# The recurrent branch's projection over both token halves by seven half-size products in rounds, with the first half's output projection ahead of the last two rounds

## The chip, the core and the metric

The kernel runs on one NeuronCore of a Trainium2 chip. The engines are TensorE (PE in the profile; PEld is its weight load), VectorE (DVE), ScalarE (ACT), GpSimd (POOL) and SyncE (SP, which here only issues DMAs). The metric is the device time of one execution in microseconds. Two kernels are compared by the medians of several executions of each.

## The reference

One layer of a decoder trunk on 1024 tokens of width 1024. The part that is changed lies between the three branches of the token mixer and the output projection:

```python
y_pool = pool_branch(...) @ w_proj_pool[l]
y_mem = mem_attention(...) @ w_proj_mem[l]
y_rwkv = rwkv_branch(...) @ w_proj_rwkv[l]
gates = jax.nn.sigmoid(z_gate.reshape(B, S, N_BRANCH, D) + gate_b[l])
merged = gates[:, :, 0] * y_pool + gates[:, :, 1] * y_rwkv + gates[:, :, 2] * y_mem
x = x + rms_norm(merged @ w_o[l], norm_mix_post[l])
```

`w_proj_rwkv` and `w_o` are 1024 x 1024. A convolutional feed-forward (width 2816, twice) follows.

## The kernel before

Activations lie with channels on the 128 partitions and tokens along the free axis; 1024 channels are 8 blocks, and the 1024 tokens are two halves of 512. For precision each factor is split into a high part in fp32r and a low part (`split`, L123, for activations; `split_w`, L127, for weights: ACT casts `whi` at L132, POOL makes `wlo` at L139), and a block of 128 x 128 weights against 128 x 512 activations takes three matmuls (`mm3`: L180 high by high, L181 high weights by low activations, L182 low weights by high activations). `gemm` sums 8 such blocks into one PSUM bank: 24 matmuls for 128 output channels of one half. `load_w` brings weights in tiles of two blocks through buffers of two classes that alternate from one load to the next: three raw tiles, four `whi` and four `wlo` in each class.

Stages around the change, in the program's order:

- the memory branch's projection (`w_pmem`, L1062 to L1070): 8 x 2 products of 12 matmuls, each multiplied with its gate into `pm` (L1070);
- the pooling branch's projection (`w_ppool`, to L1080): the same, added to `pm`;
- `yr` (L1093) loads the recurrent branch's output from DRAM, 8 blocks over all tokens, and `split` makes `yh`, `yl`;
- `merge(n, js)`: for half n and output block j, `gemm` of `w_prwkv[j]` against `yh`, `yl`, the gate's sigmoid, then on DVE L1109 (gate times PSUM), L1110 (plus `pm`) and the split into `mgh` (L124, ACT) and `mgl` (L125, DVE);
- `wo_gemm(n, js)`: the output projection; each product is copied out on DVE (L1332) and its square summed (ACT L1306, DVE L1307). The first two output blocks are woven (`two_gemms`), so that the last input block is needed late;
- `wo_residual(n)`: a matmul with ones for the norm (L1312), then for each of 8 blocks a scaling (L1355), a sum with the input (L1357), a store, and the sum of squares;
- `wo_norm(n)`: the feed-forward's norm and split into `h2h`, `h2l`; then the feed-forward's up projection.

The driver runs `merge` for half 0, `wo_gemm(0)`, `merge` for half 1 with `wo_residual(0)` woven into it, and `wo_gemm(1)` with `wo_norm(0)` inside. Every engine works its queue in order. The order within a queue is set when the program is built, from the order of the code and a scheduler's own estimate of times; a tile's buffer is reused when its last reader is done, and an instruction that waits for that holds up what stands behind it on its engine.

In the later stage (`up_pairs`) the kernel already uses the scheme that the change brings here: a 2 x 2 product of blocks by seven products and sums in place of eight products (its low halves of weights are L1172).

## Time and profile before

| | us |
|---|---|
| median of 3 runs (1959.63 to 1962.59) | 1961.81 |
| profiled execution | 1961.22 |
| its span in the trace | 1959.5 |
| TensorE busy | 1912.1 |
| DVE, ACT, POOL busy | 1361.5, 1044.3, 791.9 |

The span is what the trace covers, from the first to the last instruction. A row of a group reads: line, engine, operation, output and inputs with their shapes, count, then busy time in us and mean ns, then the engine's idle time just before them and what ended it. A row of a line's or tile's instructions gives min/median/max in ns and the first and last start in us. Rows of stretches give busy us (and instructions) for PE, PEld, DVE, ACT and POOL, the granted clock of TensorE, the DMA engines' share and GB/s.

### The profile page before, as it was taken

How to read it: one execution, taken by the hardware profiler on the slowest of the kernel's cores; microseconds unless marked ns; L12 is line 12 of the kernel's file. 1: busy time of each engine (PE TensorE's matmuls, PEld its weight loads, DVE VectorE, ACT ScalarE, POOL GpSimd, SP SyncE). 2: the span in 40 equal slices, each digit the busy share in tenths (PEclk: the TensorE clock that was granted, in tenths of full speed). 3: DMA queues.
4: the chain of work that ended last, by engine and by line, in shares of the span. 5: the costliest groups of instructions: out<-in, count | busy, mean ns of one | idle time of the engine just before them, and what ended most of it. 6: DMA issues, size and time to landing. Idle time of an engine off the chain costs nothing.

```text
span 1959.5 us, 33751 instructions
## 1 busy us (share of the span) xinstructions
PE 1912.1 (98%) x12204; PEld 1543.9 (79%) x12204; DVE 1361.5 (69%) x2022; ACT 1044.3 (53%) x2158; POOL 791.9 (40%) x867
## 2 busy tenths in 40 slices
PE   8999999999999999999999999999999999999997
PEld 6777777777777777777888888888888888888886
DVE  8677567677677435546884443689798888877798
ACT  7685385385384244445665244546554545454544
POOL 4422221321321211111223365565599888822441
PEclk9999999999999999999999999999999999999999
DMA  4325235225239668966318343644322222289775
GB/s 162 129 71 177 96 86 175 90 86 175 94 107 279 190 207 279 300 215 212 108 59 274 123 144 111 225 150 133 122 76 87 81 87 76 97 241 227 172 182 146
DMA packets 269639, 296.26 MB, mean 151 GB/s; under 512 B 18336, under 2 KB 219168, under 8 KB 266400
## 3 DMA queue, kind: packets, MB, share of 16 engines
q1 hardware_dynamic: 248480, 271.56, 43.2%
q0 software_dynamic: 11856, 14.16, 4.4%
q10 hardware_dynamic: 9136, 8.39, 1.4%
q8 instruction: 96, 1.57, 0.3%
q14 instruction: 71, 0.58, 0.1%
HBM read 207.00 MB, written 87.03 MB: 150 GB/s over the span
## 4 chain that ended last, share of the span: by engine, by line
PE 77%; DVE 8%; DMA 6%; ACT 4%; issue 3%; POOL 1%; SPq 0%; ACTq 0%; POOLq 0%; DVEq 0%
PE psg L180 14%; PE psg L182 14%; PE psg L181 14%; PE psf L182 5%; PE psf L180 5%; PE psf L181 5%; PE psd L181 3%; PE psd L182 3%; PE psd L180 3%; PE py L770 2%; DMA wraw<-in_w_in 1%; PE ps L605 1%; DVE tb L651 1%; DVE tb L653 1%; DMA d_bv<-kv 1%
## 5 line engine op out<-in xcount | busy, mean ns | idle before, releaser
L139 POOL TENSOR_TENSOR wlo<-wraw,whi 128x256 fp32r<-128x256 f32 x464 | 410.7, 897 | 833.8 <-ACT whi L132 772.7
L180 PE MATMUL psg<-hh,whi 128*128 128x512 f32 x928 | 380.1, 410 | 12.2 <-ACT whi L132 5.9
L182 PE MATMUL psg<-hh,wlo 128*128 128x512 f32 x928 | 368.0, 397 | 2.7 <-POOL wlo L139 2.2
L181 PE MATMUL psg<-hl,whi 128*128 128x512 f32 x928 | 367.8, 396 | 0.7 <-DVE hl L266 0.6
L132 ACT CAST whi<-wraw 128x256 fp32r<-128x256 f32 x472 | 181.2, 402 | 236.2 <-PE psg L181 99.1
L180 PEld LDWEIGHTS psg<-hh,whi 128*128 128x128 f32 x928 | 175.0, 189 | 60.1 <-ACT whi L132 11.2
L182 PEld LDWEIGHTS psg<-hh,wlo 128*128 128x128 f32 x928 | 175.0, 189 | 44.8 <-POOL wlo L139 7.2
L181 PEld LDWEIGHTS psg<-hl,whi 128*128 128x128 f32 x928 | 175.3, 189 | 40.5 <-issue 4.5
L1172 POOL TENSOR_TENSOR wt<-a,wt 128x256 fp32r<-128x256 f32 x136 | 155.6, 1168 | 35.1 <-ACT wt L1171 35.1
L181 PE MATMUL psd<-f,u 128*128 128x512 f32 x292 | 113.9, 390 | 0.2 <-DVE f L1588 0.2
L180 PE MATMUL psd<-f,u 128*128 128x512 f32 x292 | 113.2, 391 | 0.8 <-ACT f L1584 0.8
L182 PE MATMUL psd<-f,u 128*128 128x512 f32 x292 | 113.7, 389 | 0.0
L182 PE MATMUL psf<-h2h,wt 128*128 128x512 f32 x272 | 105.9, 389 | 0.0
L181 PE MATMUL psf<-h2l,wt 128*128 128x512 f32 x272 | 105.8, 389 | 0.0
L180 PE MATMUL psf<-h2h,wt 128*128 128x512 f32 x272 | 105.8, 389 | 0.0
L1186 DVE SCALAR_TENSOR_TENSOR d<-z,pv,d 128x1023 f32<-128x1023 f32 x68 | 101.2, 1491 | 2.1
L1172 POOL TENSOR_TENSOR wt<-s,wt 128x256 fp32r<-128x256 f32 x68 | 80.0, 1197 | 3.8 <-ACT wt L1171 2.6
L180 PE MATMUL psf<-t,wt 128*128 128x512 f32 x204 | 79.4, 389 | 0.0
L181 PE MATMUL psf<-t,wt 128*128 128x512 f32 x204 | 79.4, 389 | 0.0
L182 PE MATMUL psf<-t,wt 128*128 128x512 f32 x204 | 79.4, 389 | 0.0
L1184 ACT ACTIVATE d<-z,pv 128x1024 f32<-128x1024 f32 x34 | 42.4, 1246 | 65.3 <-DVE z L1266 49.8
L1171 ACT CAST wt<-a 128x256 fp32r<-128x256 f32 x136 | 50.6, 404 | 41.3 <-POOL wt L1172 25.9
(432 smaller groups left out, 4565.7 us busy)
## 6 DMA issues: line engine op xcount, KB each, us to landing
wraw<-in_w_in SPq DMA_DIRECT2D x176, 128.0 KB, 2.3
a<-in_w_fup SPq DMA_DIRECT2D x128, 128.0 KB, 2.3
d_ar<-AR SPq DMA_DIRECT2D x24, 512.0 KB, 3.7
d_zg<-st SPq DMA_DIRECT2D x48, 256.0 KB, 3.7
ring<-d_ar SPq DMA_DIRECT2D x8, 1536.0 KB, 10.5
wraw<-in_w_fup SPq DMA_DIRECT2D x80, 128.0 KB, 2.4
fraw<-d_f SPq DMA_DIRECT2D x33, 256.0 KB, 4.2
d_rb<-RB SPq DMA_DIRECT2D x16, 512.0 KB, 3.9
```

The source lines that it names most:

```text
L132: i = A.copy(hi, src)
L139: (V if lo_on_dve[0] else G).tensor_tensor(lo, src, hi.bitcast(F32), op=ALU.subtract)
L180: first = PE.matmul(ps, wh, xh, start=start, stop=False)
L181: PE.matmul(ps, wh, xl, start=False, stop=False)
L182: last_mm[0] = PE.matmul(ps, wl, xh, start=False, stop=stop).ins
L605: PE.matmul(ps[:, c], BK[i][up, c0 + c], AR[up, i, 1:3, t], start=True, stop=True)
L651: V.tensor_tensor(tm, X[:, s + 1:, s:s + 1].broadcast_to([P, n, m]), S[:, s:s + 1, 0:m].broadcast_to([P, n, m]), op=ALU.mult)
L770: m = PE.matmul(out_, l, r, **kw)
L1171: A.copy(w[0][:, us], src[u])
L1172: low = eng.tensor_tensor(w[1][:, us], src[u], w[0][:, us].bitcast(F32), op=ALU.subtract)
L1184: A.activation(d, z, AF.Identity, scale=col("cw2", j), bias=col("cb", j))
L1186: V.scalar_tensor_tensor(d[:, n:], z[:, :T - n], col(cw, j), d[:, n:], op0=ALU.mult, op1=ALU.add)
```

## The change

The weights (output blocks 0 to 3 and 4 to 7, input blocks 0 to 3 and 4 to 7) and the recurrent output (input blocks, token halves) are taken as 2 x 2 matrices of quarters. Seven products of quarters, each a round r = 0 to 6 with four output blocks p = 0 to 3 of 12 matmuls, give all four result quarters after sums. Rounds 0, 1 and 4 use plain quarters of the weights; rounds 2, 3, 5 and 6 use sums that are made at run time (`merge_weights`: L1158 on POOL, L1159 on DVE, L1163 on POOL; `later_weights`: L1147 and L1148 on POOL), from raw blocks of 128 x 512 in five buffers named `sw`. The activation panels are quarters of `ys` ("a" and "c" are the first half's blocks 0 to 3 and 4 to 7, "b" and "d" the second half's) or differences of them; the `A` tiles of rounds 0 and 1 are taken over by the panels of rounds 3 and 4 (`big_panels`). The weights of a product are prepared three products ahead (`rounds`).

Rounds 0 and 1 are woven, then rounds 2, 3 and 4: 20 products, after which half 0 is complete. Then comes `wo_gemm(0)` with `known_part` and `later_weights` woven in, then rounds 5 and 6 (8 products) with `wo_residual(0)` beside them, then `wo_gemm(1)`, which now takes the input blocks in the order 4 to 7, 0 to 3, and copies its results out on ACT. The tiles of the `at` pool are now halves of 512 tokens.

```diff
+    y_ctx = ExitStack()
+    yp = y_ctx.enter_context(tc.tile_pool(name="yp", bufs=1, side="right"))
+    ys = {}
+
+    for k in range(4):
+        for nm, e, h in (("a", 0, 0), ("c", 4, 0), ("b", 0, 512), ("d", 4, 512)):
+            ys[nm, k] = yp.tile([P, 512], F32, name=f"y{nm}{k}", tag=f"y{nm}{k}")
+            SP.dma_start(ys[nm, k], d_y[e + k][:, h:h + 512])
+    big = [yp.tile([P, 4, 512], FR, name=f"yp{m}", tag=f"A{m}") for m in range(4)]
     for j in range(8):
+        if j % 2:
+            k = j // 2
+            split(ys["a", k], big[0][:, k], big[1][:, k], V)
+            split(ys["c", k], big[2][:, k], big[3][:, k], V)
+            V.tensor_tensor(ys["a", k], ys["b", k], ys["a", k], op=ALU.subtract)
+            V.tensor_tensor(ys["b", k], ys["d", k], ys["b", k], op=ALU.subtract)
+            G.tensor_tensor(ys["c", k], ys["c", k], ys["d", k], op=ALU.subtract)
+            G.tensor_tensor(ys["c", k], ys["c", k], ys["a", k], op=ALU.add)
         ws = load_w(w_ppool[j], 4)
...
+    def gated_sum(j, n, src, add, eng):
+
+        gt = gts[j, n]
+        V.tensor_tensor(gt, src, gt, op=ALU.mult)
+        V.tensor_tensor(gt, gt, add, op=ALU.add)
+        mgh[j, n] = half_tile(j, n, "mgh")
+        mgl[j, n] = pmp.tile([P, 512], FR, name=f"mgl{j}{n}", tag=f"n{2 * j + n}")
+        split(gt, mgh[j, n], mgl[j, n], eng)
+
+    def known_part(j):
+
+        c = result(j, 1)
+        later(V.tensor_tensor(c, c, gts[j, 1], op=ALU.mult), last_mm[0])
+        V.tensor_tensor(c, c, pm[j][1], op=ALU.add)
...
+    def raw_weights(j, k0):
+        w = mq.tile([P, 4, P], F32, name="sw", tag="sw", bufs=5)
+        SP.dma_start(w, w_prwkv[j][:, k0:k0 + 4])
+        return w
+
+    def later_weights(p):
+
+        s1[p], y = raw_weights(4 + p, 0), raw_weights(4 + p, 4)
+        later(G.tensor_tensor(s1[p], s1[p], y, op=ALU.add), last_mm[0])
+        G.tensor_tensor(kept[p], raw_weights(p, 4), kept[p], op=ALU.subtract)
+
+    def merge_weights(r, p):
+
+        plain_ = {0: (p, 0), 1: (p, 4), 4: (4 + p, 4)}.get(r)
+        if plain_:
+            return load_w(w_prwkv[plain_[0]][:, plain_[1]:plain_[1] + 4], 4)
+        if r == 2:
+            x, y, z = raw_weights(4 + p, 0), raw_weights(4 + p, 4), raw_weights(p, 0)
+            src = kept[p] = mq.tile([P, 4, P], F32, name=f"S{p}")
+            G.tensor_tensor(src, x, y, op=ALU.add)
+            V.tensor_tensor(src, src, z, op=ALU.subtract)
+            corner[0] = z, x
+        elif r == 3:
+            src, y = corner[0]
+            G.tensor_tensor(src, src, y, op=ALU.subtract)
+        else:
+            src = (s1 if r == 5 else kept)[p]
...
+        if r == 0:
+            A.copy(result(p, 0), ps)
+            A.copy(u2, ps)
+        elif r in (1, 4):
+            j = p if r == 1 else z
+            c = result(j, 0)
+            V.tensor_tensor(c, c, ps, op=ALU.add)
+            gated_sum(j, 0, c, pm[j][0], V)
+        elif r == 2:
+            V.tensor_tensor(u2, u2, ps, op=ALU.add)
+        elif r == 3:
+            V.tensor_tensor(result(z, 0), u2, ps, op=ALU.add)
+            A.copy(result(z, 1), result(z, 0))
+        elif r == 5:
+            first_sum[p] = wp.tile([P, 512], F32, name="m1", tag="st", bufs=3)
+            A.copy(first_sum[p], ps)
+            gated_sum(z, 1, ps, result(z, 1), G)
+        else:
+            V.tensor_tensor(first_sum[p], first_sum[p], ps, op=ALU.add)
+            gated_sum(p, 1, first_sum[p], u2, V)
...
-    merge(0, range(8))
-    wo_gemm(0, range(8))
-    merge(1, range(1))
-    pin = last_mm[0]
-    merge(1, range(1, 3))
+    merge(6)
+    big_panels(3, "b", 0)
+    merge(2)
+    big_panels(4, "c", 2)
+    gates_of([yp.tile([P, 512], F32, name="g1", tag=f"yb{k}") for k in range(4)], 4, 0)
+    merge(12)
+    small_panels(5, "a", "bc")
+    big_panels(6, "d", 0)
+    for j, nm in ((4, "a"), (0, "d")):
+        gates_of([yp.tile([P, 512], F32, name="g1", tag=f"y{nm}{k}") for k in range(4)], j, 1)
+    for p in range(4):
+        wo_gemm(0, range(2 * p, 2 * p + 2))
+        known_part(4 + p)
+        known_part(p)
+        later_weights(p)
     table(LN_EXP)
-    res = wo_residual(0, pin)
+    merging = rounds(woven(5, 6))
+    merge(2)
+    res = wo_residual(0, last_mm[0])
```

In the rows below, the lines of the changed kernel are: L1125 and L1126 the gate's product and sum in `gated_sum`, L1189 the sum of rounds 1 and 4 with PSUM, L1201 that of round 6, L1217 the difference of `second_panels`; `yp` are the panels of rounds 3 and 4; L1487 and L1489 are what L1355 and L1357 were.

POOL before, around the recurrent projection: 213 low halves of weights in a row, from the memory branch's projection to the feed-forward.

```order
L139 TENSOR_TENSOR wlo<-wraw,whi 128x256 x8
L139 TENSOR_TENSOR ulo<-uraw,uhi 128x128
L139 TENSOR_TENSOR wlo<-wraw,whi 128x256 x4
L139 TENSOR_TENSOR ulo<-uraw,uhi 128x128
L139 TENSOR_TENSOR wlo<-wraw,whi 128x256 x213
```

POOL now, in rounds 0 to 2, from the first difference L1163 to the first L1148 (S_11843, S_11916, S_12027 and S_12116 are the summed weights for output blocks 0 to 3).

```order
L1163 TENSOR_TENSOR sw<-sw 128x512
L139 TENSOR_TENSOR wlo<-wraw,whi 128x256
L1158 TENSOR_TENSOR S_11916<-sw 128x512
L1163 TENSOR_TENSOR sw<-sw 128x512
L139 TENSOR_TENSOR wlo<-wraw,whi 128x256
L139 TENSOR_TENSOR wlo<-S_11843,whi 128x256 x2
L1158 TENSOR_TENSOR S_12027<-sw 128x512
L139 TENSOR_TENSOR wlo<-sw,whi 128x256
L1163 TENSOR_TENSOR sw<-sw 128x512
L139 TENSOR_TENSOR wlo<-sw,whi 128x256
L1158 TENSOR_TENSOR S_12116<-sw 128x512
L139 TENSOR_TENSOR wlo<-S_11916,whi 128x256 x2
```

Behind the last of these rows stand two low halves, the fourth L1163, the first L1148, and then the two low halves of round 4's first product. The sums have come between the low halves that TensorE waits for.

DVE before, in the first half's `merge` (each number behind a name is a buffer's).

```order
L1109 TENSOR_TENSOR g_11696<-g_11696,psg 128x512
L1110 TENSOR_TENSOR g_11696<-g_11696,pm_10799 128x512
L1109 TENSOR_TENSOR g_11704<-g_11704,psg 128x512
L125 TENSOR_TENSOR mgl_11701<-g_11696,mgh_11587 128x512
L1110 TENSOR_TENSOR g_11704<-g_11704,pm_10801 128x512
```

DVE now, in rounds 0 and 1, from the second difference L1159 to the first low parts of round 3's panel.

```order
L1159 TENSOR_TENSOR S_11916<-S_11916,sw 128x512
L125 TENSOR_TENSOR mgl_11773<-g_11618,mgh_11772 128x512
L1189 TENSOR_TENSOR sum_11741<-sum_11741,psr 128x512
L1125 TENSOR_TENSOR g_11619<-sum_11741,g_11619 128x512
L1159 TENSOR_TENSOR S_12027<-S_12027,sw 128x512
L1126 TENSOR_TENSOR g_11619<-g_11619,pm_10809 128x512
L125 TENSOR_TENSOR mgl_11834<-g_11619,mgh_11833 128x512
L125 TENSOR_TENSOR yp<-yb_11186,yp 128x512
L125 TENSOR_TENSOR yp<-yb_11194,yp 128x512
```

The weight differences stand among the evacuations, and the panel's low parts behind them. On ACT the cast of g_11619 and two copies out of PSUM stand between there and the casts of that panel.

DVE before, in the second half's `merge`, from the first scaling of the residual on.

```order
L1355 SCALAR_TENSOR_TENSOR o<-o,pv,rs 128x512 x2
L1357 TENSOR_TENSOR o<-o,xt 128x512 x2
L1355 SCALAR_TENSOR_TENSOR o<-o,pv,rs 128x512 x2
L1307 TENSOR_TENSOR s_12658<-s_12658,sq 128x512
L1109 TENSOR_TENSOR g_12698<-g_12698,psg 128x512
L1355 SCALAR_TENSOR_TENSOR o<-o,pv,rs 128x512
L1110 TENSOR_TENSOR g_12698<-g_12698,pm_10806 128x512
```

DVE now, in rounds 5 and 6, from the first scaling on.

```order
L1487 SCALAR_TENSOR_TENSOR o<-o,pv,rs 128x512 x2
L1489 TENSOR_TENSOR o<-o,xt 128x512 x2
L1201 TENSOR_TENSOR m_12853<-m_12853,psr 128x512
L1487 SCALAR_TENSOR_TENSOR o<-o,pv,rs 128x512
L1441 TENSOR_TENSOR s_12895<-s_12895,sq 128x512
L1125 TENSOR_TENSOR g_12320<-m_12853,g_12320 128x512
L1125 TENSOR_TENSOR g_12310<-psr,g_12310 128x512
L1126 TENSOR_TENSOR g_12320<-g_12320,sum_11711 128x512
```

The residual's rows, 8 blocks of them, now alternate with those of 8 products of 12 matmuls, where they lay among 5 of 24.

149 lines of the change are left out of this document (92 added, 57 removed).

## Prediction

> **What bounds the kernel now.** I read the page first, then the busy times by stretch (cut where the stages begin and end), the waits of TensorE, and last the rows of the instructions that the change adds.
>
> ```profile
> span 1959.5 us, 33751 instructions
> PE 1912.1 (98%) x12204; PEld 1543.9 (79%) x12204; DVE 1361.5 (69%) x2022; ACT 1044.3 (53%) x2158; POOL 791.9 (40%) x867
> ```
>
> The stretches are: recurrent projection of the first half, output projection of the first half, recurrent projection of the second half, output projection of the second half, and the start of the feed-forward. Columns: PE, PEld, DVE, ACT and POOL busy (instructions), granted clock, DMA share, GB/s.
>
> ```profile
> 1120.10:1163.60 43.50, 43.50 (x193) 36.04 (x192) 22.87 (x27) 21.31 (x50) 27.34 (x33) 1.00 0.44 143
> 1163.60:1207.10 43.50, 43.50 (x193) 36.05 (x192) 11.64 (x17) 18.37 (x43) 25.03 (x34) 1.00 0.35 113
> 1207.10:1251.50 44.40, 44.40 (x195) 36.39 (x194) 31.63 (x45) 25.40 (x52) 22.97 (x29) 1.00 0.59 189
> 1251.50:1296.40 44.90, 44.90 (x197) 36.81 (x197) 29.10 (x37) 20.04 (x50) 27.39 (x32) 1.00 0.47 154
> 1296.40:1400.00 103.60, 103.17 (x449) 83.89 (x449) 89.34 (x139) 61.45 (x136) 62.06 (x74) 1.00 0.45 145
> ```
>
> TensorE is full in every stretch, at full clock, and no other engine is over two thirds in the first two. The only thing that TensorE itself waited for in 1120 to 1300 is this:
>
> ```profile
> PE psn L1312 <- DVE ss L1336: 0.2, 1, 0.2
> ```
>
> So here time is matmuls, and a matmul taken out is time gained, unless TensorE has to wait for what replaces it. What one costs is not its duration. First the group of the projection's first product (128 of its 384), then three neighbours in the timeline:
>
> ```profile
> L180 PE MATMUL psg<-yh,whi 128*128 128x512 f32 x128 | 50.2, 392 | 0.0
> 1284.66 0.39 PE L180 MATMUL psg<-mgh,whi 128*128 128x512 f32 x1
> 1284.89 0.39 PE L181 MATMUL psg<-mgl,whi 128*128 128x512 f32 x1
> 1285.12 0.39 PE L182 MATMUL psg<-mgh,wlo 128*128 128x512 f32 x1
> ```
>
> Each lasts 0.39 us, but one starts every 0.2266 us: 43.50 us for 192 in the first stretch. They overlap, and the spacing is the price.
>
> **What goes.** Before: 16 products of 24 matmuls, 384. After: 7 rounds of 4 products of 12, 336. 48 x 0.2266 = **10.9 us less** on TensorE; the order bears out the count. At the mean duration it would be 18.8 us, which is wrong for the reason just shown. The rows after this part stand in the same order as before, and TensorE is 98% busy to the end, so I let a microsecond gained or lost here reach the end whole.
>
> **What is added** lies on POOL, DVE, ACT and SP: sums of weights and of panels, more splits, more evacuations. The prices, POOL first. The rows are the low halves in the projection's first stretch and over the whole kernel, and the only plain 128x512 sum on POOL:
>
> ```profile
> L139 POOL TENSOR_TENSOR wlo<-wraw,whi 128x256 fp32r<-128x256 f32 x33 | 28.2, 871 | 19.6 <-ACT whi L132 13.5 <-PE psg L182 2.7 <-DMA wraw<-in_w_prwkv 2.2
> L139 POOL TENSOR_TENSOR wlo<-wraw,whi x464: 722/742/2971, 5.7 to 1392.8; 128x256 fp32r<-128x256 f32 x155
> L1625 POOL TENSOR_TENSOR ss<-ss,sq 128x512 f32<-128x512 f32 x6 | 9.0, 1494 | 12.1 <-ACT sq L1623 12.1
> L1625 POOL TENSOR_TENSOR ss<-ss,sq x6: 1282/1420/1926, 1831.3 to 1903.9; 128x512 f32<-128x512 f32 x6
> ```
>
> DVE, in min/median/max and then as means in 1207.1 to 1296.4:
>
> ```profile
> L1109 DVE TENSOR_TENSOR g<-g,psg x16: 673/684/689, 1130.0 to 1253.9; 128x512 f32<-128x512 f32 x16
> L1110 DVE TENSOR_TENSOR g<-g,pm x16: 684/1010/1253, 1130.8 to 1254.6; 128x512 f32<-128x512 f32 x16
> L125 DVE TENSOR_TENSOR mgl<-g,mgh 128x512 fp32r<-128x512 f32 x8 | 7.5, 939 | 5.5 <-ACT mgh L124 5.5
> L1110 DVE TENSOR_TENSOR g<-g,pm 128x512 f32<-128x512 f32 x8 | 7.1, 890 | 0.1
> L1357 DVE TENSOR_TENSOR o<-o,xt 128x512 f32<-128x512 f32 x8 | 6.5, 838 | 1.4 <-DMA xt<-in_xT 1.4
> L1355 DVE SCALAR_TENSOR_TENSOR o<-o,pv,rs 128x512 f32<-128x512 f32 x8 | 5.8, 741 | 0.0
> L1307 DVE TENSOR_TENSOR s<-s,sq 128x512 f32<-128x512 f32 x7 | 4.8, 679 | 0.2 <-ACT sq L1306 0.2
> ```
>
> ACT (whi, a gate's sigmoid, a cast of 128x512, a copy out of PSUM), and the gates' loads of 256 KB: SP's issue, and from issue to landing:
>
> ```profile
> L132 ACT CAST whi<-wraw x472: 383/405/418, 5.2 to 1405.2; 128x256 fp32r<-128x256 f32 x158
> L214 ACT ACTIVATE g<-g x24: 616/633/1062, 1031.0 to 1243.5; 128x512 f32<-128x512 f32 x16, 128x1024 f32<-128x1024 f32 x8
> L124 ACT CAST mgh<-g x16: 615/619/622, 1132.6 to 1257.9; 128x512 fp32r<-128x512 f32 x16
> L1248 ACT COPY z<-psf x17: 577/585/589, 1416.4 to 1719.1; 128x512 f32<-128x512 f32 x17
> L1106 SPq DMA_DIRECT2D g<-d_zg x16: 326/327/431, 1052.7 to 1239.4; - x16
> DMA to landing us min/median/max: 2.5/3.1/5.6
> ```
>
> So, bare and as a mean: a low half 0.74 and 0.87 us, a POOL sum of 128x512 1.28 and 1.49, a DVE operation on two SBUF tiles 0.68 and about 0.93, on PSUM 0.68; a cast 0.62, a copy 0.58; a load 2.5 or 3.1, with 0.4 to issue it.
>
> **First wait, rounds 2 to 4.** t counts from round 0's first matmul; product n (0 to 19) would start at 2.72n, which is 12 x 0.2266. Queues run in order, so I walk them. ACT gets to product 5's high halves at about t = 11: ahead of them stand four whi (1.6 us), four casts of the panel e (2.5), four sigmoids (2.5) and four copies (2.3), and waits for product 0 and for the gates' loads, which I put at 2. From there POOL has, in this order of the rows, up to and with the third L1158: eight low halves and four sums (the first two L1163, the second and third L1158), and between the second L1158 and the second L1163 it waits for L1159 on DVE: 8 x 0.87 + 4 x 1.49 + 0.93 = 13.9, so t = 24.9 (bare 22.7). DVE stands at the third L1159 for it: 25.8. Behind that stand L1126 of g_11619 (26.7), ACT's cast of it (27.4), two copies (28.5), and only then round 3's panel: four casts of 0.62 and the low parts on DVE, the last at 32.9. Product 9, round 3's first, is due from 24.5 to 27.2 and ends at 33.4: 6.2 us late (bare 2.3).
> The second link: the third L1163 ends at 27.3, and it frees the buffer into which the second block of the fourth L1158 is loaded: landed at 30.8, fourth L1158 32.3, four low halves 35.8, fourth L1163 37.3. This one frees the buffer of L1148's block: landed at 40.8, L1148 42.3, low half of product 12 (round 4's first) at 43.1, where TensorE would want it at 33.1 (32.6 and two matmuls). That is 10.0 us late in all, the 6.2 within it (bare: 38.0, 4.9 late). I take **8.5 us**, nearer to the mean, as POOL and DVE are fuller than in the stretch that gave the means. Later products gain nothing back, since TensorE is what limits them.
>
> **Second wait, from the last two rounds into the second output projection.** U is round 5's start. TensorE needs 8 x 2.72 + 0.86 for the sum of squares = 22.6, and the order puts 48 matmuls ahead of the last mgl: wanted at 33.5. The residual's first scaling comes about 3 us after that sum's matmul:
>
> ```profile
> L1312 PE MATMUL psn<-ss,ones x6: 592/592/697, 1223.7 to 1925.0; 128*128 128x512 f32 x6
> L1355 DVE SCALAR_TENSOR_TENSOR o<-o,pv,rs x16: 732/742/748, 1226.7 to 1321.9; 128x512 f32<-128x512 f32 x16
> ```
>
> So U + 5.4 + 3.0 = 8.4. From it to the last mgl DVE has 40 rows: 8 scalings, 7 residual sums, 5 sums of squares, 4 L1201, 6 L1125 (two on PSUM), 6 L1126, 4 mgl = 5.9 + 5.9 + 3.4 + 2.7 + 4.9 + 5.3 + 3.8 = 31.9 us, bare 27.7: U + 36.1 to 40.3, so TensorE waits 2.6 to 6.8 us. Before, the same residual lay beside 43.5 us of matmuls, now beside 22. I take **5 us**.
>
> **At nothing:** known_part and later_weights lie under the first output projection, where DVE had 11.6 and POOL 25 us of 43.5 in use; without that cover 16 DVE operations, 15 us, and 8 POOL sums, 12 us. The copy of o moves from DVE (0.68) to ACT (0.58), which has the room that the fourth stretch shows. The weights loaded grow from 8.4 MB (16 blocks of 128x1024) to 9.4 (36 of 128x512), at a DMA share of 0.44. The panels of rounds 0 and 1 are made under the memory branch (third rival).
>
> **Sum.** The profiled execution took 1961.22 us, its span and 1.7 around it; the median, 1961.81, is 0.6 higher, and I add to the median: -10.9 + 8.5 + 5 = +2.6, **1964.4 us**. With both waits bare -3.4, with both at the means +5.9: 1958.4 to 1967.7 is this case's own range. A measurement of this kernel tells about 0.2% (3.9 us) from no change.
>
> **A rule against the change.** L1109, which reads one tile from PSUM, never leaves 0.68; L1110, with both in SBUF, goes up to 1.25, and POOL's low half from 0.74 to 0.87 in the mean.
> The Trainium skill, SBUF — State Buffer, section Who interferes with whom, says that a DVE instruction with two SBUF inputs and a GpSimd instruction that reads SBUF exclude each other for their whole length. The two DVE rows agree with it. By it the first wait would be that of the second rival.
>
> **Rivals.**
> 1. The waits stay short (0.23): the block for L1148 is there in time and prices are bare. Then 2.3 + 2.6 are left: -6.0, 1955.8. For it: idle time in the queues that I may have missed, and loads of 2.5. Against: the addresses of the blocks chain the loads to the sums.
> 2. POOL and DVE hold each other up (0.18): the roughly 20 DVE operations on two SBUF tiles in t = 11 to 43 take 13.6 us bare; if half of it falls in POOL's way, 4.9 + 6.8 = 11.7, with 6.8 at the second wait +7.6, 1969.4. It decides from an overlap of 3.1 us on (4.9 + 3.1 + 6.8 - 10.9 = 3.9). For it: L1110. Against: POOL's low halves stay at 0.87 in the mean, where every one held up would be at 0.74 + 0.68.
> 3. The y panels choke the memory branch (0.07). Its 16 products start here, its loads end here:
>
> ```profile
> L180 PEld LDWEIGHTS psg<-oh,whi x64: 187/188/188, 1033.1 to 1075.9; 128*128 128x128 f32 x64
> 1046.37 0.91 SPq L1067 DMA_DIRECT2D pm<-d_zg  x2
> ```
>
> A PSUM bank comes round every fourth product; the multiply of the twelfth now stands behind 19 panel operations and 5 multiplies, from about 1053 (1047.3, a load, casts): at 0.93, 1074.1 + 0.7, wanted at 1033.1 + 15 x 2.72 = 1073.9; at L1110's median 1.01 2.4 us late. On top of the forecast: +5.0, 1966.8.
> That the change does less than it says is excluded by the count of matmuls in the order.
>
> **Chances.** Forecast 0.52 (no change 0.34, slower 0.18), first rival 0.23 (faster 0.22, no change 0.01), second 0.18 (slower), third 0.07 (no change 0.05, slower 0.02): faster 0.22, no change 0.40, slower 0.38. The range reaches from the first rival to a little over the second: 1955.5 to 1971.5.
>
> **What would show it.** 48 matmuls fewer, still 0.2266 us apart outside the waits. TensorE waits at the first product of round 3 for ACT or DVE (panel), and at the first of round 4 for POOL (wlo), 5 to 10 us together; then at mgh and mgl of blocks 2 and 3, 2.6 to 6.8 us. The third L1159 begins at t = 23 to 25. If TensorE has no idle time over 2 us in t = 24 to 44, the walk is wrong and the time near 1956; if it waits in 1033 to 1076, the third rival is at work.

## The result, and the profile after

The changed kernel takes 1985.05 us (median of 6, 1983.09 to 1989.64), the kernel before beside it 1962.16 (1959.63 to 1966.79). The ratio is 1.012, with a 95% interval of 1.0102 to 1.0137: slower by 22.9 us. The forecast was 1964.4 with a range to 1971.5, so the loss is far outside.

The page of the changed kernel has the matmuls as forecast, 12204 - 12156 = 48 fewer, but TensorE has fallen from 98% to 96% of a longer span.

```profile
span 1982.9 us, 33824 instructions
PE 1912.9 (96%) x12156; PEld 1538.8 (78%) x12156; DVE 1406.4 (71%) x2079; ACT 1059.3 (53%) x2196; POOL 837.4 (42%) x887
```

The same stretches as in the prediction, each from its stage's first matmul to the next stage's: memory and pooling branches; rounds 0 to 4; first output projection; rounds 5 and 6; second output projection; start of the feed-forward. Columns: length, then PE, PEld, DVE, ACT and POOL busy (instructions), granted clock, DMA share, GB/s.

```profile
1032.54:1123.06 90.52, 87.58 (x386) 71.92 (x384) 49.52 (x63) 31.14 (x61) 38.21 (x39) 1.00 0.54 177
1123.06:1194.33 71.27, 59.25 (x242) 46.19 (x241) 50.45 (x62) 39.69 (x89) 51.73 (x50) 0.95 0.52 163
1194.33:1239.59 45.26, 44.33 (x194) 35.80 (x193) 25.40 (x34) 21.37 (x51) 32.94 (x36) 1.00 0.43 134
1239.59:1264.27 24.68, 23.14 (x100) 18.16 (x98) 21.70 (x28) 14.34 (x31) 23.36 (x21) 1.00 0.25 78
1264.27:1315.75 51.48, 47.26 (x194) 37.18 (x195) 35.15 (x48) 28.94 (x67) 28.94 (x35) 0.97 0.60 195
1315.75:1430.83 115.08, 112.56 (x485) 90.21 (x484) 93.90 (x153) 66.36 (x144) 64.03 (x77) 1.00 0.40 127
```

PE is no longer equal to the length, and in two stretches the clock is below 1.00. At 0.2266 us a matmul rounds 0 to 4 would take 240 x 0.2266 = 54.4: they lose 16.9. What TensorE waited for between 1000 and 1430, the six largest rows (total us, times, longest):

```profile
PE psr L182 <- POOL wlo L139: 7.0, 5, 3.1
PE psg L180 <- ACT mgh L124: 3.1, 2, 1.9
PE psg L180 <- DVE pm L1073: 2.9, 2, 2.3
PE psr L180 <- ACT whi L132: 2.8, 2, 2.6
PE psr L180 <- ACT yp L124: 2.7, 1, 2.7
PE psn L1446 <- DVE ss L1441: 1.5, 1, 1.5
```

The first row (but for 0.7 of it, which lies in round 5), the fourth and the fifth are the first wait of the prediction, the second is the second wait, the third is the third rival, all at once. The whole difference of the two spans, 1982.9 - 1959.5 = 23.4, comes out stage by stage ("bare" is the count of matmuls at 0.2266, and 0.9 for each sum of squares):

| stage | before | after | bare, with the change | lost |
|---|---|---|---|---|
| memory and pooling branches | 87.0 | 90.5 | 87.0 | 3.5 |
| recurrent projection of half 0 / rounds 0 to 4 | 43.5 | 71.3 | 54.4 | 16.9 |
| first output projection | 43.5 | 45.3 | 43.5 | 1.7 |
| projection of half 1 / rounds 5 and 6, and second output projection | 88.9 | 76.2 | 67.1 | 9.1 |
| start of the feed-forward | 112.2 | 115.1 | 112.2 | 2.9 |

34.1 lost, less 10.9 for the 48 matmuls, and 0.2 in all that lies before and behind: 23.4.

### The profile page after: what moved, and what is told of

Same layout as the page of the kernel before. It is cut to its first block, busy times and chain, and to the rows that moved or that the text cites. A ratio compares the mean times of both kernels' runs of the same rounds, so it can differ in the third digit from the quotient of the medians.

```text
span 1982.9 us, 33824 instructions
## 1 busy us (share of the span) xinstructions
PE 1912.9 (96%) x12156; PEld 1538.8 (78%) x12156; DVE 1406.4 (71%) x2079; ACT 1059.3 (53%) x2196; POOL 837.4 (42%) x887
## 4 chain that ended last, share of the span: by engine, by line
PE 68%; DVE 13%; DMA 7%; ACT 5%; issue 4%; POOL 3%; SPq 0%; POOLq 0%; ACTq 0%; DVEq 0%
PE psg L180 11%; PE psg L182 10%; PE psg L181 10%; PE psf L182 5%; PE psf L180 5%; PE psf L181 5%; PE psd L181 3%; PE psd L180 3%; PE psd L182 3%; POOL wlo L139 2%; PE py L770 2%; DMA wraw<-in_w_in 1%; DVE tb L651 1%; DVE tb L653 1%; PE ps L605 1%
## 5 line engine op out<-in xcount | busy, mean ns | idle before, releaser
L139 POOL TENSOR_TENSOR wlo<-wraw,whi 128x256 fp32r<-128x256 f32 x424 | 385.7, 923 | 787.7 <-ACT whi L132 752.0
L180 PE MATMUL psg<-hh,whi 128*128 128x512 f32 x928 | 381.1, 411 | 11.8 <-ACT whi L132 5.2
L132 ACT CAST whi<-wraw 128x256 fp32r<-128x256 f32 x432 | 165.7, 403 | 207.5 <-PE psg L181 94.6
```

The costliest lines, as they stand in the source:

```text
L132: i = A.copy(hi, src)
L139: (V if lo_on_dve[0] else G).tensor_tensor(lo, src, hi.bitcast(F32), op=ALU.subtract)
L180: first = PE.matmul(ps, wh, xh, start=start, stop=False)
```

## The experiments

Each kernel was profiled once and timed in three rounds beside the kernel before. This table has the stages of the profiled execution (the last two rows of the stage table, rounds 5 and 6 with the output projection, are one column) and the medians' difference to the kernel before of the same call. Stages that an experiment doesn't touch scatter by up to 5 us (the start of the feed-forward, 115.1 to 119.7 from the changed kernel to e3), mostly with the clock (below), so an edit is judged by its own stage first.

| kernel | memory, pooling | rounds 0-4 | 1st output | rounds 5-6, 2nd output | feed-forward | to before |
|---|---|---|---|---|---|---|
| changed | 90.5 | 71.3 | 45.3 | 76.2 | 115.1 | +22.9 |
| e1 panels later | 87.0 | 71.3 | 44.7 | 75.8 | 116.2 | +18.5 |
| e2 no sums | 92.1 | 56.2 | 45.5 | 73.9 | 116.8 | +11.8 |
| e3 loads earlier | 89.8 | 67.5 | 46.7 | 75.4 | 119.7 | +25.0 |
| e4 residual late | 89.6 | 71.0 | 47.4 | 79.7 | 114.5 | +26.2 |
| e5 difference early | 93.3 | 67.6 | 45.1 | 75.6 | 118.3 | +25.9 |
| e6 filled waits | 92.0 | 68.1 | 46.1 | 75.2 | 115.8 | +25.8 |
| e7 residual spread | 90.9 | 71.2 | 45.0 | 74.8 | 114.8 | +22.2 |
| e8 sums on DVE | 91.7 | 60.1 | 50.2 | 76.2 | 117.8 | +17.3 |
| e9 no residual | 91.1 | 71.0 | 50.1 | 70.3 | 118.2 | +25.6 |
| e10 all mended | 87.0 | 61.5 | 49.6 | 75.6 | 114.1 | +11.4 |
| e11 all, difference early | 87.0 | 67.7 | 43.6 | 75.0 | 117.0 | +15.0 |
| e12 order mended | 87.0 | 63.1 | 47.1 | 78.0 | 115.7 | +18.1 |
| e13 order, three sums | 87.0 | 64.4 | 46.7 | 76.1 | 120.6 | +17.3 |

My theory after the result: the sums in POOL's queue make the low halves late (first wait), DVE's queue makes the last gated sums late (second wait), the panels hold up the memory branch, and each wait costs more than its length because the clock falls behind it. The rivals: late loads; engines that hold each other up; products of 12 matmuls that are too short for their own evacuations.

### e1: the panels behind the memory branch

```diff
-            split(ys["a", k], big[0][:, k], big[1][:, k], V)
-            split(ys["c", k], big[2][:, k], big[3][:, k], V)
+            later(split(ys["a", k], big[0][:, k], big[1][:, k], V), last_mm[0])
+            later(split(ys["c", k], big[2][:, k], big[3][:, k], V), last_mm[0])
```

> Of the changed kernel, the splits and differences that make the panels of rounds 0 and 1 are ordered behind the memory branch's last product; nothing else is edited. If the third rival is right (they stand on DVE ahead of the memory branch's evacuations L1073, and TensorE waits 0.68 + 2.27 us for those), the stretch from the memory branch's first matmul to the projection's first is 86.8 us again, as before the change, in place of 90.5, no wait for pm is left, and the time falls by 3.7 us, from 1985 to about 1981. If DVE only hands the backlog on, the pooling branch or round 0 waits for it and the time stays within 1 us of 1985.

The stretch is full again, to the hundredth what it was before:

```profile
1033.03:1120.07 87.04, 87.04 (x386) 72.07 (x385) 49.34 (x63) 32.74 (x64) 33.43 (x36) 1.00 0.57 185
```

The third rival is shown, 3.5 us. In DVE's timeline of the changed kernel one sees why: differences of the panels, two SBUF tiles each, at up to 1.4 us, and behind them four evacuations at once, for the first of which TensorE has waited.

```profile
1071.23 1.38 DVE L1088 TENSOR_TENSOR ya<-yb,ya 128x512 f32<-128x512 f32 x1
1072.54 1.22 DVE L1217 TENSOR_TENSOR t<-yd,ya 128x512 f32<-128x512 f32 x1
1073.68 1.22 DVE L1089 TENSOR_TENSOR yb<-yd,yb 128x512 f32<-128x512 f32 x1
1074.83 1.21 DVE L1217 TENSOR_TENSOR t<-yd,ya 128x512 f32<-128x512 f32 x1
1075.96 2.47 DVE L1073 TENSOR_TENSOR pm<-pm,psg 128x512 f32<-128x512 f32 x4
```

### e2: no sums of weights

```diff
-        plain_ = {0: (p, 0), 1: (p, 4), 4: (4 + p, 4)}.get(r)
+        plain_ = {0: (p, 0), 1: (p, 4), 2: (4 + p, 0), 3: (p, 0), 4: (4 + p, 4)}.get(r)
...
-        G.tensor_tensor(kept[p], raw_weights(p, 4), kept[p], op=ALU.subtract)
+        kept[p] = raw_weights(p, 4)
```

> Of the changed kernel, the weight sums of rounds 2 and 3 (L1158, L1159, L1163) and of L1148 are left out: these rounds use plain quarters of the weights, loaded like those of rounds 0, 1 and 4, so the output isn't the reference's. Splits, panels, matmuls and evacuations stay. In the changed kernel the 240 matmuls of rounds 0 to 4 take 71.3 us where 54.4 would do: 16.9 lost. If the sums and their loads are the cause, 2 to 5 us stay lost (panel casts, single low halves), no granted clock under 1.00 is left there, and the time falls by 12 to 15, to about 1971. If the panels and the splits of twelve-matmul products are the cause whatever the weights are, over 10 stay lost and the time stays over 1978.

```profile
1124.87:1181.06 56.19, 55.48 (x242) 44.74 (x240) 42.60 (x56) 38.40 (x86) 35.79 (x39) 1.00 0.58 174
```

71.3 became 56.2: the sums and what they wait for are 15.1 of the 16.9. Panels, casts and short products alone cost 1.8. Even so this kernel, which leaves work out, is 11.8 us slower than before (ratio 1.0065, 1.0049 to 1.0082).

### e3: the loads of the sums earlier

```diff
+    summands(0)
+    summands(1)
     merging = rounds(...
...
-            x, y, z = raw_weights(4 + p, 0), raw_weights(4 + p, 4), raw_weights(p, 0)
-            G.tensor_tensor(src, x, y, op=ALU.add)
+            src, x, z = summands(p)
+            G.tensor_tensor(src, x, src, op=ALU.add)
```

> Of the changed kernel, the raw blocks for the sums of output blocks 0 and 1 are loaded ahead of round 0's weights, and one of the three blocks of each sum goes straight into the sum's own tile, so that five buffers last for two and a half sums. The sums stay where they were on POOL and DVE. First theory (the loads come late: the first L1158 waited 6.8 us for its block, the first L1148 2.8): the first L1158 starts by t = 10 where it was 14.1, 6 to 10 of the 16.9 us lost in rounds 0 to 4 go, time about 1977. Second theory (POOL and DVE have too much to do there, POOL was 84% busy in 1140 to 1180, and hold each other up): the first sum starts earlier, but 12 or more stay lost, time 1980 or more.

The first sum began at 1138.77, t = 13.1, and not by 10: these blocks were issued only at 1133.2, t = 7.5, hardly earlier than before (t = 8.3). So the kernel didn't do what it was made for, and settles little: what earlier blocks alone would bring, no run shows. The stretch fell by 3.8.

### e4: the residual behind the rounds

```diff
-    for j in range(6):
-        merge(1)
-        s2 = next(res, s2) if j % 2 else s2
+    merge(6)
...
+    wo_gemm(1, range(1))
+    res = wo_residual(0, last_mm[0])
+    for j in range(1, 4):
+        s2 = next(res)
+        wo_gemm(1, range(j, j + 1))
```

> Of the changed kernel, the first half's residual is made beside the first four output blocks of the second output projection (its norm behind the first), and no longer beside rounds 5 and 6. If DVE's backlog from the residual is the second wait, the stretch from round 5's first matmul to the feed-forward's first loses the waits for mgh and mgl and its 3.4 us of half clock: 76.2 us becomes 68 to 70, and the time falls by 5 to 8 to about 1979, unless the norm that follows the residual waits longer than its 1.5 us, which could give back up to 5. If the backlog is rounds 5 and 6 themselves (each product has a sum, a product with the gate, a sum and a split), the stretch stays over 74 us.

The waits of rounds 5 and 6 go (21.8 us, the bare count) and of those for mgh and mgl behind them 1.8 are left of 4.2, but the norm gives back more than I allowed for:

```profile
PE psn L1446 <- DVE s L1441: 6.8, 1, 6.8
PE psg L181 <- POOL mgl L125: 1.3, 1, 1.3
...
PE psg L180 <- ACT mgh L124: 0.5, 1, 0.5
```

So the residual is what makes the last products late, and moving it makes the next stage late instead.

### e5: z - x beside the pooling branch

```diff
+            x, z = (half_tile(4 + k, n, "w", F32)...)
+            SP.dma_start(x, w_prwkv[4 + k][:, 0:4])
+            SP.dma_start(z, w_prwkv[k][:, 0:4])
+            G.tensor_tensor(z, z, x, op=ALU.subtract)
...
-            G.tensor_tensor(src, x, y, op=ALU.add)
-            V.tensor_tensor(src, src, z, op=ALU.subtract)
+            V.tensor_tensor(src, src, corner[p], op=ALU.subtract)
```

> Of the changed kernel, x + y - z is made as y - (z - x): the difference z - x of the weights, which round 3 needs anyway, is made on POOL already beside the pooling branch, in tiles that the memory branch has done with, and rounds 2 to 4 keep one sum for each output block (on DVE) in place of three; the four late raw blocks for them are no longer loaded there. The output stays the reference's up to rounding. Theory: the three sums on POOL and DVE, and the buffers that their loads wait for, are what makes rounds 0 to 4 lose 16.9 of their 71.3 us; leaving all sums out got the stretch to 56.2. Then it is 57 to 60 here, no granted clock under 1.00 in it, and the time 1985 - 12 = about 1973. Rival: the panel's casts and the splits of round 3 stand at the same place whatever the sums are, and the new work beside the pooling branch holds up TensorE there: stretch over 64, or the pooling branch 2 us longer; time 1980.

My forecast for it failed: 67.6 in place of 57 to 60, and 2.8 more in the memory and pooling branches, as its rival had it (over 64, or 2 more). Part of the 2.8 is a stretch at half clock from 1077 on, which e2, where nothing is edited there, has too. The waits in rounds 0 to 4 are no longer POOL's in the main:

```profile
PE psr L180 <- ACT whi L132: 4.9, 2, 2.6
PE psr L182 <- POOL wlo L139: 1.6, 2, 1.1
PE psr L180 <- DVE g L1104: 1.2, 2, 0.7
```

ACT's timeline shows where it stood. The sigmoids of the first gates wait for their loads, which stand on SP behind weight loads, which wait for buffers; copies and the next high halves are queued behind them:

```profile
1137.55 1.30 ACT L214 ACTIVATE g<-g 128x512 f32<-128x512 f32 x2 [3.59 <-DMA g<-d_zg]
1138.76 0.60 ACT L124 CAST e<-t 128x512 fp32r<-128x512 f32 x1
1139.27 0.63 ACT L214 ACTIVATE g<-g 128x512 f32<-128x512 f32 x1
...
1142.22 1.65 ACT L132 CAST whi<-wraw 128x256 fp32r<-128x256 f32 x5
```

TensorE had waited 2.6 for the first of those five. Taking work off POOL helps only as far as ACT's queue.

### e6: matmuls in two of the waits

```diff
+        for _ in range({(4, 0): 10, (3, 0): 10}.get((r, p), 0)):
+            PE.matmul(ps, panel[2](0)[0][:, :P], panel[2](1)[0], start=True, stop=True)
         for k in range(4):
             mm3(ps, w[k], panel[r](k), k == 0, k == 3)
```

> Of the changed kernel, 10 more matmuls of 128x512 (2.3 us, into the PSUM bank that the next product overwrites, on a panel that is already there) stand ahead of the first product of round 3 and of the first product of round 4, where TensorE waits 2.7 and 2.6 us in any case. Theory: a wait that leaves TensorE idle through most of a stretch of 3.41 us halves its granted clock for the next one or two such stretches (the record: 0.50 for 6.83 us right behind the wait at 1165.6 to 1168.4), and this costs 2 to 3.4 us on top of the wait. Then the granted clock stays 1.00 in rounds 0 to 4 and the stretch falls from 71.3 to 68 to 69, the time to about 1982. Rival: the clock has nothing to do with the wait, or the other waits around it are enough to halve it: 0.50 is still there, and the stretch is 71 to 73.

Twenty matmuls more, and the stretch is 68.1, 3.2 shorter; the granted clock is 0.97 in it and not 1.00, since a wait of 3.1 for POOL ahead of the filled ones still halved it, for one stretch of 3.41 us in place of two. The stretch fell as expected, but not for that reason alone: the wait at product 5, which the edit doesn't touch, is 0.2 us here and was 1.7, and one stretch of half clock fewer is worth only about 0.9. So this run doesn't show the price of the clock. The median didn't move either, as half clocks turned up in other stages; e14 and e15 measure the price.

### e7: half of the residual beside the output projection

```diff
-        s2 = next(res, s2) if j % 2 else s2
+        s2 = next(res, s2) if j == 3 else s2
...
-    wo_gemm(1, range(4))
+    for j in range(4):
+        wo_gemm(1, range(j, j + 1))
+        s2 = next(res, s2) if j < 2 else s2
```

> Of the changed kernel, two of the residual's four steps (of two blocks each) stay beside rounds 5 and 6 and two move beside the first output blocks of the second output projection. With all four beside the rounds, the last split of round 6 came 1.9 + 1.2 + 1.1 us too late and then half a clock; with all four behind them the norm came 6.8 us too late. Theory (DVE has 40 rows in a line there, and whatever stands first makes the other late): rounds 5 and 6 with the second output projection, 76.2 us, come to 71 to 74, and the time falls by 2 to 5. Rival (the rows are all needed at the same point, so that only the name of the wait changes): 75 to 78, time 1984 to 1987.

74.8, 1.3 less than 76.2, with a wait of 2.8 for mgh left. Neither theory's range holds clearly.

### e8: the sums on DVE

```diff
-            G.tensor_tensor(src, x, y, op=ALU.add)
+            V.tensor_tensor(src, x, y, op=ALU.add)
...
-            G.tensor_tensor(src, src, y, op=ALU.subtract)
+            V.tensor_tensor(src, src, y, op=ALU.subtract)
```

> Of the changed kernel, the sums L1158 and L1163 are moved from POOL (1.43 and 1.58 us each, eight of them, 12 us) to DVE (0.68 to 1.2 each), so that POOL makes nothing but low halves in rounds 0 to 4. Theory (POOL's queue is what is late, 84% busy in 1140 to 1180): the stretch of rounds 0 to 4 falls from 71.3 to 63 to 67, time 1977 to 1981. Rival (DVE and POOL hold each other up, so that work moved between them gains nothing, and DVE's evacuations come late as well): 70 to 74, time 1984 or more.

The same work on another engine, and 11.2 of the 16.9 us are gone, more than I expected. Rounds 0 to 4 and the first output projection:

```profile
1124.58:1184.64 60.06, 56.76 (x242) 46.00 (x240) 49.21 (x62) 34.86 (x81) 41.37 (x41) 0.97 0.56 175
1184.64:1234.80 50.16, 47.18 (x193) 37.35 (x192) 29.51 (x41) 24.33 (x57) 33.56 (x38) 0.93 0.46 140
```

DVE is no busier in it (49.2 for 50.5): L1159 takes 0.79 in the mean in place of 1.08, and work moved on to the next stretch: four of a panel's low parts (2.7) and the evacuation of one product more. That L1159 is shorter because fewer of POOL's operations lie beside it is likely, but not shown. But that stretch lost 5: the waits there are for high halves (1.9) and mgh (1.0) on ACT, whose queue stood for 1.8 us at sigmoids of the second half's gates, and the clock halved behind them. The gain in time is 5.6 us, 22.9 to 17.3.

### e9: no residual

```diff
+            if n or k == 0:
                 V.scalar_tensor_tensor(o[k], o[k], col("g_mix_post", k), rs, ...
                 V.tensor_tensor(o[k], o[k], xt, op=ALU.add)
...
+            if n or k == 0:
                 sumsq(s2, o[k], k == 0, V)
```

> Of the changed kernel, the first half's residual is left out for seven of its eight blocks (L1487, L1489 and the squares' sums L1441: 21 rows on DVE, some 17 us, and seven squares on ACT), so the output isn't the reference's; its loads, stores, the norms and everything of rounds 5 and 6 stay. Theory (the second wait is DVE's queue, which holds 40 rows from the residual's first to the last split of round 6): without them rounds 5 and 6 and the second output projection, 76.2 us where the matmuls fill 67.1, come to 67 to 69, and the time falls by 6 to 9 to 1976 to 1979. Rival (the twelve-matmul products of rounds 5 and 6 come too fast for their own evacuations, residual or not): 72 us or more, time over 1981.

Rounds 5 and 6 and the second output projection fell from 76.2 to 70.3, by 5.9 of the 9.1 that they lose; 1.3 and 0.9 are left for mgl and mgh. That is between theory and rival, nearer to the theory. The time didn't fall: with no rows to wait for, all eight of the residual's loads of its input are issued by 1194 (1273 in the changed kernel), among the second half's gates, whose sigmoids then hold up ACT for 4.2 us, and the first output projection waits 3.5 us for an mgh behind them:

```profile
ACT g L214 <- DMA g<-d_zg: 4.2, 2, 3.2
...
PE psg L180 <- ACT mgh L124: 3.5, 1, 3.5
```

### e10 and e11: all of it together

```diff
-            G.tensor_tensor(src, x, y, op=ALU.add)
-            V.tensor_tensor(src, src, z, op=ALU.subtract)
+            V.tensor_tensor(z, z, x, op=ALU.subtract)
+            V.tensor_tensor(src, y, z, op=ALU.subtract)
...
-    gates_of([ow.tile(...) for g in ("ss", "ss", "xt", "xt")], 0, 0)
...
-    merge(6)
+    merge(1)
+    gates_of([ow.tile(...) for g in ("ss", "ss", "xt", "xt")], 0, 0)
+    merge(5)
```

with the edits of e1 and e7 and the second half's gates behind the first two output blocks; e11 makes the difference as e5, on DVE.

> Of the changed kernel, several edits together: the panels of rounds 0 and 1 behind the memory branch; x + y - z made as y - (z - x), two sums in place of three, both on DVE; the first gates' loads behind round 0's first product and the second half's behind the first two output blocks; half of the residual beside the second output projection. The output stays the reference's up to rounding. From the runs before: 3.5 less before the projection, rounds 0 to 4 at 58 to 61 in place of 71.3, the first output projection back to 44 to 45 (with the sums on DVE alone it had gone to 50, with the second half's gates ahead of the weights' casts on ACT), 1 less behind: 1985 - 3.5 - 11 - 1 - 1 = about 1968, still slower than before, as the waits that remain (4 to 6 us in rounds 0 to 4, 7 behind, 3 in the feed-forward's start) are more than the 10.9 of the matmuls. Rival: the lost time moves on to the next stage each time; then 1975 or more.

> As the kernel with all edits together, but with z - x made beside the pooling branch, on DVE, which is half idle there, and not on POOL, where it held up the low halves and, through them, the loads: in rounds 2 to 4 only one sum for each output block is left. If the sums are what is left of the first wait, rounds 0 to 4 come to 56 to 59, the time to about 1966. If what is left are the loads and casts that stand in line ahead of them on SP and ACT (the gates, the panel), then it is the same as there within 2 us.

e10 is the fastest that still computes the layer: 1973.91 us (ratio 1.0053, 1.0036 to 1.007), still 11.4 slower than before. That is between its forecast (1968) and its rival (1975 or more). Its rounds 0 to 4 are close to the forecast (61.5 for 58 to 61), its first output projection (49.6 for 44 to 45) isn't: TensorE waits 2.6 for mgh there, and one stretch of 3.4 us runs at half clock. e11 loses again in rounds 0 to 4 what it gains behind them: 67.7 is neither of its two forecasts. Its waits there are mostly ACT's (whi 4.1), as in e5.

### e12 and e13: another order

```diff
+            if r == 1 and p:
+                waiting.append((j, 0, c, pm[j][0], V))
+            else:
+                gated_sum(j, 0, c, pm[j][0], V)
...
     big_panels(3, "b", 0)
+    gated_sum(*waiting.pop(0))
```

and, behind the first two output blocks by an order on ACT, the panels of rounds 5 and 6 and the second half's gates; three steps of the residual later, the norm one block later. e13 is the same with the three sums of the change, on DVE.

> Of the changed kernel, as the kernel with all edits (panels behind the memory branch, two sums on DVE), but the first gates stay where they were, and three things are put in another order: the gates' sums of round 1's second to fourth product stand behind the panel casts of rounds 3 and 4 and no longer ahead of them; the panels of rounds 5 and 6 and the second half's gates stand behind the first two output blocks; three of the residual's four steps lie beside the second output projection, and the norm behind them comes one block later. The output stays the reference's up to rounding. Theory (what is left is the order in which ACT and DVE take their rows, not their amount): rounds 0 to 4 at 56 to 58 (61.5 with all edits, a wait of 2.9 for the panel's casts and 3.4 us of half clock), the first output projection at 44 (49.6, with a wait of 2.6 for mgh and 3.4 us of half clock), rounds 5 and 6 with the second output projection at 70 to 73 (75.6): 1974 - 4 - 5 - 3 = about 1962, level with before. Rival (ACT and DVE are too full between 1122 and 1310, whatever the order): the waits change their names and the time stays over 1970.

> As the kernel with the mended order, but with the three sums of the change (x + y, - z, and z - x) in place of two, all on DVE: 12 sums there in place of 8, some 4 us more on DVE in rounds 0 to 4. If DVE's amount of work counts there, the stretch is 2 to 4 longer than with two sums; if its order does, the two are within 1.

The rival held, with 1979.31 us, and no stage of e12 came to its forecast. The wait for the panel's cast on ACT (2.9) became one for its low part on DVE (3.5); mgh is awaited for 2.7 in the second output projection, as for 2.8 in e7. e13 is 1.3 us longer than e12 in rounds 0 to 4, between its two forecasts (2 to 4, or within 1), so whether the number of sums on DVE counts stays open; it isn't the larger part.

### e14 and e15: what a wait costs

The kernel before, with waits put behind six products of its full first output projection (m = 0 in e14, 3 in e15):

```diff
+                V.tensor_copy(t, ps)
+                for _ in range(m):
+                    V.tensor_tensor(t, t, t, op=ALU.max)
+                V.tensor_copy(d, t)
+                held[0] = PE.matmul(pss.tile(...), mgh[0][:, :P], d, start=True, stop=True).ins
```

> The kernel before, with waits put into its full first output projection: behind each of six products DVE copies the result out twice (about 0.7 us and under 0.7), and one more matmul of 128x512 on that copy stands ahead of the next product, so TensorE waits some 1.5 us at four places at least. Nothing else is changed, and the output stays the reference's. It measures the price of a wait by itself. Theory: each costs the wait as reported, 0.2266 for the matmul, and 0.2 to 0.4 us until the spacing is full again; too short to halve the granted clock, which stays 1.00 in 1160 to 1210: 6 x 2.0 = 8 to 12 us more, 1970 to 1974. Rival: such short waits, 5.4 us apart, halve it already: 0.50 shows there, and the cost is over 14.

> As the kernel with short waits, but with three more operations of 0.7 us on DVE in each chain: TensorE waits some 3.5 us at each place. Theory: a stretch of 3.41 us in which TensorE is idle for most of it is followed by one or two of half clock; 3.5 us of wait in every 9 leave most of such a stretch idle about half of the time, so that two to four stretches of 0.50 show in 1160 to 1220, each costing 1.7 us, on top of 6 x 4.0 = 24: 27 to 32 us more, 1988 to 1994. Rival (the clock does not follow the waits): no 0.50 there, 22 to 25 us more.

e14 takes 14.5 us more than before, e15 33.8, both a little over what I expected. From the first output projection's start to the feed-forward's, where the edit lies, the two take 142.4 and 164.2 us where the kernel before takes 132.4: 10.0 and 31.8 more, within both forecasts. Of the rest of e14, 3.4 is in the start of the feed-forward (115.6 for 112.2). TensorE waits at four of the six places, in e14 for 1.7 to 1.8 us, in e15 for 4.5 to 5.1 where I had 3.5. In e14 a wait of 1.7 leaves the clock at 1.00, and the matmuls are back at 0.23 after two:

```profile
1191.89 0.50 PE L1338 MATMUL psn<-t,mgh 128*128 128x512 f32 x1 [1.71 <-DVE t L1337]
1192.22 0.40 PE L180 MATMUL psg<-mgh,whi 128*128 128x512 f32 x1
1192.46 0.39 PE L181 MATMUL psg<-mgl,whi 128*128 128x512 f32 x1
```

From one added matmul to the next are 7.68 us, where 25 x 0.2266 = 5.67 would do: 2.0 for a wait that is reported as 1.7. In e15 the same distance is 12.89, 13.33 and 11.89 for waits of 4.5, 4.6 and 4.6: 7.2, 7.7 and 6.2. Its stretches of 3.4 us, length, PE busy, and granted clock:

```profile
1175.30:1178.70 3.40, 0.00 (x0) 1.00 0.37 116
1178.70:1182.10 3.40, 1.71 (x4) 0.51 0.12 39
1182.10:1185.50 3.40, 3.40 (x9) 0.50 0.02 5
1185.50:1189.00 3.50, 3.27 (x14) 0.99 0.22 75
```

So the clock follows the waits: a stretch of idleness, one or two at half clock, and full again; seven stretches of half clock in all where I expected two to four.

## Why the prediction was wrong

By its own steps:

- **What goes, 10.9: right.** 48 matmuls fewer, 0.2266 apart outside the waits and half clocks.
- **First wait: right mechanism, size off, 16.9 for 8.5.** The walk named the queue (POOL's, with the sums between the low halves), the panel and the links: TensorE waited for whi and wlo at product 5, for wlo at product 7, for the panel at product 9 and for whi and wlo at product 12. The step that failed is its start, "ACT gets to product 5's high halves at about t = 11", with POOL's rows going on from there. The high halves came at 1136.50, t = 13.4, as ACT stood 4.0 us for the gates' loads, where I had put 2 for them and product 0. And the first sum, which I had taken as done by then, stood ahead of the low halves and waited for its block to t = 14.2, so that they began at t = 15.4. Part of both is the price of a load: SP issued the gates, two weight tiles and five blocks for the sums from 1127.36 to 1133.6, and they landed 3.5 to 5.8 us after their issue, where I had 2.5 or 3.1. POOL's rows, and the longest wait of TensorE for them, at product 7:

```profile
1137.21 1.28 POOL L1158 TENSOR_TENSOR S<-sw 128x512 f32<-128x512 f32 x1 [6.82 <-DMA sw<-in_w_prwkv]
1138.45 4.17 POOL L139 TENSOR_TENSOR wlo<-wraw,whi 128x256 fp32r<-128x256 f32 x4
...
1149.46 0.50 PE L182 MATMUL psr<-yp,wlo 128*128 128x512 f32 x1 [3.11 <-POOL wlo L139]
1150.76 1.28 POOL L1158 TENSOR_TENSOR S<-sw 128x512 f32<-128x512 f32 x1
```

  The third L1158 ended at 1152.0, t = 29.0, where I had 24.9: 13.6 behind the first sum's end, for 13.9 in the walk. From there the walk's intervals hold within 1.2: the fourth L1163 ended 13.6 later (walk 12.4), and L1148 then waited 2.77 for its block, as the second link has it. TensorE got product 12's high half 45.3 after the start and its low half at 47.8 (walk 43.1). So the low half came 14.7 late, where the walk's mean gave 10.0 and I took 8.5; the half clock (next) makes up about the rest. That the third L1159 would begin at 23 to 25 was wrong by the same 4: 1152.07, t = 29.0.
- **The clock: left out.** I wrote "at full clock" and priced waits at their length. Here is TensorE at product 12:

```profile
1165.36 0.39 PE L182 MATMUL psr<-yp,wlo 128*128 128x512 f32 x1
1168.37 0.80 PE L180 MATMUL psr<-yp,whi 128*128 128x512 f32 x1 [2.62 <-ACT whi L132]
1168.96 0.63 PE L181 MATMUL psr<-yp,whi 128*128 128x512 f32 x1
1170.89 0.80 PE L182 MATMUL psr<-yp,wlo 128*128 128x512 f32 x1 [1.29 <-POOL wlo L139]
1171.48 0.63 PE L180 MATMUL psr<-yp,whi 128*128 128x512 f32 x1
1171.91 0.63 PE L181 MATMUL psr<-yp,whi 128*128 128x512 f32 x1
```

  Matmuls 0.43 apart, to 1175: some 2.5 us in this stretch, and about 1.6 more in the 3.41 us from 1277.5 on in the second output projection. Each wait costs about 0.3 more besides (e14).
- **Second wait: right mechanism, size off, 9.1 for 5.** From the first scaling to the last mgl DVE took 1250.4 to 1281.3, 30.9 us for the 40 rows, and 31.9 was the walk's mean. It began 2.4 later than U + 8.4, and the half clock and the 2.0 us that rounds 5 and 6 lost themselves (24.7 for 22.6) came on top. e9 puts 5.9 us on the residual.
- **Third rival: came true as well.** Priced at 2.4, it cost 3.5 (e1). I had made it an alternative with a chance of 0.07. It had nothing to do with the first wait, so it was a term of the sum.
- **At nothing: not quite.** known_part and later_weights were covered, but the first output projection lost 1.7 and the feed-forward's start 2.9, half of it (1.5) a wait for the second half's squares.
- **Second rival, POOL and DVE in each other's way.** Its rows are there: L1159, on two SBUF tiles, had 0.69 at the least and 1.20 at the median, and the mean low half came to 1.0 in rounds 0 to 4, from 0.87.

```profile
L1159 DVE TENSOR_TENSOR S<-S,sw x4: 692/1200/1218, 1138.5 to 1159.8; 128x512 f32<-128x512 f32 x4
L139 POOL TENSOR_TENSOR wlo<-wraw,whi 128x256 fp32r<-128x256 f32 x24 | 23.9, 1019 | 7.8 <-ACT whi L132 7.7
```

  The rule of the Trainium skill (SBUF — State Buffer, Who interferes with whom) agrees with these rows. It isn't what makes the stage late, as far as the runs tell: from the first sum's end to the third's POOL took 13.6 us, where the walk has 11.7 with bare prices and 13.9 with means, so the means already held it. And with the sums moved to DVE (e8), where by the rule they exclude POOL all the same, 11.2 us went.

With 3.5 for the memory branch, 16.9, 9.1 and 4.6 in the terms I had at 0, 8.5, 5 and 0, the sum is 23.2 in place of 2.6. What stays open is whether any order of these queues keeps TensorE fed: e10 to e13 each mended one wait and found the next, and no version tried beats the kernel before.

## What to carry to other kernels

- A matmul taken out of a full stretch is worth its spacing; a wait put in costs its length, 0.3 more, and 1 to 3 more if it empties over half of a stretch of 3.41 us. Shorter products bring more rows for the other engines per matmul, so ask first whether those queues have room.
- Begin the walk of a queue at the load that its first row waits for, on the engine that issues it, and not at the first row. Here the order and landing of SP's loads set when ACT's sigmoids and POOL's first sum could run, and POOL's queue set TensorE's.
- Rivals with separate causes add up. They belong into the sum with their chances, not beside it.

## What the runs showed of the hardware

The granted clock is 1.00 or 0.50, and goes to 0.50 in stretches of 3.41 us on a grid that runs through the execution. What decides is how busy TensorE was in the stretch before. In the seventeen traces, each cut on its own grid, every stretch at full clock with under 1.49 us of 3.41 busy was followed by half clock, and none with over 2.2 was. In between it went both ways, so busy time alone doesn't settle it there: 1.95 (e3, from 1157.19 on) and 1.87 (e4, from 1206.82 on) were followed by half clock, 1.58 (e7, from 1163.75 on) and 1.63 (the changed kernel, from 1072.79 on) were not. Behind a stretch at half clock it stayed at 0.50 with up to 2.79 us busy, and was 1.00 again from 2.86 on. The changed kernel around product 12, cut on that grid (length, PE busy, clock):

```profile
1161.46:1164.88 3.42, 3.42 (x16) 1.00 0.37 135
1164.88:1168.29 3.41, 0.87 (x4) 1.00 0.50 171
1168.29:1171.70 3.41, 2.04 (x4) 0.51 0.39 137
1171.70:1175.12 3.42, 3.42 (x9) 0.50 0.52 161
1175.12:1178.53 3.41, 3.41 (x16) 0.99 0.51 154
```

So the same waits cost differently in different executions: those for pm at 1071 to 1077 left 1.63 in the changed kernel's stretch and 1.14 in that of e2, which got half a clock for it (92.1 for 90.5). The Trainium skill (TensorE: Matmul & The Clock Gate, Part 1) has the gate, its two ratios and the window of 3413 ns that runs free, and the traces agree. It puts the slow state behind at least one idle window, and here one with 1.95 us of work in 3.41 was enough (e3); the measurement decides.
